# A two-layer decoder trunk: every fifth block of stick-breaking logits takes its PSUM bank from the pool of the transposes

## The chip, the cores and the metric

The kernel runs on one core of a Trainium2 chip. A core has five engines that work through their own instruction queues in order: TensorE (PE; its weight loads, PEld, overlap its matmuls), VectorE (DVE), ScalarE (ACT), GpSimd (POOL) and SyncE (SP), which here only issues DMAs. Matmuls write to PSUM, which holds eight banks of 128 partitions by 512 float32 values. The metric is the device time of one execution in microseconds (us).

## The reference

Two layers over x of 2048 tokens by 1024. Layer 0 projects to four forgetting-attention heads, four stick-breaking heads (both of width 128) and a gate; layer 1 has dilated window attention. The change touches the stick-breaking heads alone. For a block of 128 queries:

```python
strict = jnp.arange(end)[None, :] < qpos[:, None]
z = jnp.einsum('bhqd,bhkd->bhqk', q[:, :, start:end], k[:, :, :end]).astype(jnp.float32)
log_beta = jax.nn.log_sigmoid(z)
log_one_minus = jnp.where(strict, log_beta - z, 0.0)
...
w = jnp.where(strict, jnp.exp(log_beta + later), 0.0)
outs.append(jnp.einsum('bhqk,bhkd->bhqd', w.astype(v.dtype), v[:, :, :end]))
```

Here `later` is, for each key, the sum of `log_one_minus` over all later keys. So a weight is sigmoid(z) of its key times the product of sigmoid(-z) over the later keys of the row: a running product from the last key to the first.

## The kernel before

Every float32 matmul is made of three passes (lines 91 to 93, `mm3`) over operands split into a rounded high part and a low remainder. `split` makes them: ACT copies the high part (L81), DVE subtracts it for the low part (L86).

The function `even_attention` works through 64 units in order: first the stick-breaking heads ("s"), then the forgetting heads ("f"), four heads of each, eight units per head. Unit u holds 2 rows of 128 queries; row i needs the keys up to its own 128, so a unit u has 2 (u // 2 + 1) blocks of at most 512 keys: 2, 2, 4, 4, 6, 6, 8, 8, or 40 blocks per head. In each row the blocks run from the last keys to the first, because the running product is carried that way; the first block of a row is 128 to 512 keys wide, the others 512.

For one block of a stick-breaking head, `qk` takes a PSUM bank, lets PE write the logits into it (L91 to L93, and L878 adds the mask in a row's first block), and then

- ACT writes sigmoid(z) to `rows` (L889) and sigmoid(-z) back into the bank (L890),
- DVE scans the bank from right to left into `rest`, the running product (L893),
- POOL multiplies `rows` by the shifted `rest` (L896), which gives the weights.

The bank is free again after the scan. The generator `pv` of a unit runs two units later, merged with the `qk` of the unit then due: per pair of key tiles it transposes four 128 x 128 pieces of weights into one bank (L928), splits them (L81, L86) and multiplies them by the values into an output bank that it holds for the whole unit; at the end the gate is applied (L946).

The PSUM pool has two kinds of banks, "s" and "t", four each. Before the change all logits use "s"; the transposes and the stick-breaking units' output sums use "t".

The order of the instructions isn't written out. The kernel records its work in the order of the Python code, and a scheduler then orders it for each engine by priority (earlier code first) and by when it thinks operands and free banks are there. Which of a pool's banks a tile gets is decided there too. So a change of a bank's kind can reorder all engines.

Where numbers stand in names (ps_9517), they tell PSUM tiles apart.

Of the kernel before, what the change touches and what calls it, by code (L numbers as in the profile page):

```python
# [831 lines left out]
def even_attention(k, tail):  # L832
    tc, nc = k.tc, k.nc
    c2 = k.c2
    scale = float(P) ** -0.5
    heads, bias = {}, {}

    def load_head(kind, h):
        T, V = (k.fT, k.v["f"]) if kind == "f" else (k.sT, k.v["s"])
        kt = k.big([P, 4, 2, CH], F32R, name="kt")  # L840
        vt = k.big([P, 4, 2, TPC, P], F32R, name="vt")

        def chunk(c):
            s = slice(c * CH, (c + 1) * CH)
            nc.sync.dma_start(kt[:, c].bitcast(F32), T["k"][:, h, :, s].bitcast(F32))
            for z in range(2):
                nc.sync.dma_start(vt[:, c, z].bitcast(F32),
                                  V[s, z, h * P:(h + 1) * P].rearrange("(j p) d -> p j d", p=P).bitcast(F32))

        heads[kind, h] = kt, vt  # L850
        return chunk
# [11 lines left out]
    def qk(kind, h, u, q, tile, left):  # L863

        kt, vt = heads[kind, h]
        c = u // 2
        for i in range(2):
            rows = tile[:, i]
            a = [q[:, z, i * P:(i + 1) * P] for z in range(2)]
            nk = (u * 2 + i + 1) * P  # L870
            carry = None
            for kc in range(c, -1, -1):
                n = CH if kc < c else nk - c * CH
                b = kc * CH
                ps = k.ps("s")
                k.mm3(ps[:, :n], a, [kt[:, kc, z, :n] for z in range(2)], True, kc < c)
                if kc == c:
                    nc.tensor.matmul(ps[:, n - P:n], k.identb, k.after if kind == "f" else k.notbefore,  # L878
                                     start=False, stop=True)
                dst = rows[:, b:b + n]  # L880
                if kind == "f":
                    m = k.small.tile([P, 1], F32, name="m")
                    nc.vector.tensor_tensor_reduce(
                        out=dst, in0=ps[:, :n], in1=bias[h, kc][:, :n], op0=OP.add, op1=OP.max,
                        scale=1.0, scalar=3.0 * NEG if carry is None else carry, accum_out=m)
                    carry = m
                else:

                    nc.scalar.activation(dst, ps[:, :n], AF.Sigmoid, scale=scale)  # L889
                    nc.scalar.activation(ps[:, :n], ps[:, :n], AF.Sigmoid, scale=-scale)  # L890
                    o = left[:, i]
                    back = ps[:, :n][:, ::-1]
                    nc.vector.tensor_tensor_scan(o[:, b:b + n][:, ::-1], back, k.ident[:, :1].to_broadcast([P, n]),  # L893
                                                 1.0 if carry is None else carry, OP.mult, OP.bypass)
                    w = n - 1 if carry is None else n
                    nc.gpsimd.tensor_tensor(dst[:, :w], dst[:, :w], o[:, b + 1:b + 1 + w], op=OP.mult)  # L896
                    carry = o[:, b:b + 1]
                yield
            if kind == "f":
                nm = k.small.tile([P, 1], F32, name="nm")  # L900
                nc.vector.tensor_scalar(nm, carry, -1.0, None, op0=OP.mult)
                den = k.small.tile([P, 2], F32, name="den")
                cuts = [(b, min(b + 2 * CH, nk)) for b in range(0, nk, 2 * CH)]
                for z, (b, e) in enumerate(cuts):
                    nc.scalar.activation(rows[:, b:e], rows[:, b:e], AF.Exp, bias=nm,
                                         accum_out=den[:, z:z + 1])
                if len(cuts) == 2:
                    nc.vector.tensor_tensor(den[:, :1], den[:, :1], den[:, 1:], op=OP.add)
                rd = k.small.tile([P, 1], F32, name="rd")
                nc.vector.reciprocal(rd, den[:, :1])  # L910
                for b, e in cuts:
                    nc.gpsimd.tensor_scalar(rows[:, b:e], rows[:, b:e], rd, 1.0, op0=OP.mult, op1=OP.mult)
# [55 lines left out]
    for n, (kind, h, u) in enumerate(units):  # L968
        rows = k.big([P, 2, S], name="rows")
        rest = k.big([P, 2, S], name="rest") if kind == "s" else None  # L970
        gens = [(qk(kind, h, u, q, rows, rest), 2 * (u // 2 + 1))]
        if n + 1 < len(units):
            q = load_q(*units[n + 1])
        if (kind, h, u) == ("f", 0, 0):
            k.table()
        nxt = order.index((kind, h)) + 1
        if u == 1 and nxt <= 6:
            slopes((nxt - 1) // 2, (nxt - 1) % 2)
        if nxt < len(order) and u >= 3:
            if u == 3:  # L980
                chunk = load_head(*order[nxt])
            else:
                chunk(u - 4)
        if len(past) == 2:
            v = past.pop(0)
            gens.append((pv(*v[0], v[1]), v[0][2] + 1))
        merged(*gens)
        past.append(((kind, h, u), rows))
        if nxt == len(order) and u in (3, 4, 5, 7):

            tail()
# [403 lines left out]
@with_exitstack  # L1395
def tile_hybrid_trunk(ctx, tc, x, even_norm, even_w_in, even_b_f, even_q_gain, even_k_gain, even_w_out,
                      odd_norm, odd_w_in, odd_q_gain, odd_k_gain, odd_w_out, out):
    k = K(ctx, tc)
    k.table()
    x1 = k.dram.tile([S, D], F32, name="x1d")  # L1400
    A = []
    spare = []
    first = left_direct(k, x[0], even_norm, A, spare)
    next(first)
    identity(k)
    late = lambda: constants(k, k.cs, even_norm, odd_norm, even_b_f, even_q_gain, even_k_gain, odd_q_gain, odd_k_gain)
    even_projection(k, x[0], even_w_in[0], first, A, spare, late)
    odd = odd_layer(k, x[0], x1, even_w_out[0], odd_w_in[0], odd_w_out[0], out[0])
    next(odd)
    even_attention(k, lambda: next(odd))  # L1410
    next(odd, None)
# [28 lines left out]
```

## Time and profile before

| what | us |
|---|---|
| median of 3 runs (2764.96 to 2770.11) | 2767.83 |
| the profiled execution's own time | 2767.75 |
| its span, first to last instruction | 2766.0 |
| first scan of a stick-breaking block starts | 701.9 |
| last scan of a stick-breaking block starts | 995.7 |
| 160 scans, 96 of them carried from the block before in the row (L893) | 1.278 each where 512 wide and carried |

The profile is of one execution. Busy times count the instructions of an engine; a wait is the idle time of an engine ahead of an instruction, put down to the instruction that released it. Matmuls are pipelined, so a busy PE isn't a PE at its peak. The chain of waits, followed back from the last instruction, is 70% PE and 17% DVE over the whole span.

### The profile page before, as it was taken

The page shows a single profiled execution, that of the slowest core. Times are in us where ns is not written, and L with a number is a line of the kernel's source. Part 1 is how long each engine was busy: PE and PEld are TensorE (multiplying, and loading weights), DVE is VectorE, ACT ScalarE, POOL GpSimd, SP SyncE. Part 2 cuts the span into 40 slices and gives each one's busy share as a digit, 9 for nine tenths or more (in the row PEclk, how much of TensorE's full clock was granted, in tenths as well). Part 3 has the DMA queues.
Part 4 walks back from the last instruction along what each step waited for, and adds up shares of the span by engine and source line. Part 5 has one row for each costly group of instructions (what it writes and reads, how often), then busy time and mean ns, then how long its engine had stood idle before and what let it go on. Part 6 is the DMA issues. An engine that isn't in the chain of part 4 may idle for free.

```text
span 2766.0 us, 54039 instructions
## 1 busy us (share of the span) xinstructions
PE 2664.9 (96%) x19615; PEld 2418.7 (87%) x19615; DVE 1923.3 (70%) x4255; ACT 1577.2 (57%) x3843; POOL 1102.5 (40%) x903
## 2 busy tenths in 40 slices
PE   6999999999998899999999899999989999999998
PEld 5899878998787789988889899999889999999876
DVE  7867774684788887787237767475896676663976
ACT  6456654454767665665546345555663678665642
POOL 3545654544544433332004654343254432422322
PEclk9999999999999999999999999999999999999999
DMA  5576864445433334443564333444634444444675
GB/s 184 179 214 186 276 209 146 153 143 190 151 115 117 118 116 145 142 132 111 193 203 149 111 108 116 131 133 128 203 98 143 129 154 146 141 138 141 222 257 184
DMA packets 382154, 432.56 MB, mean 156 GB/s; under 512 B 30976, under 2 KB 315968, under 8 KB 381888
## 3 DMA queue, kind: packets, MB, share of 16 engines
q1 hardware_dynamic: 381888, 429.11, 48.3%
q8 instruction: 155, 2.54, 0.4%
q14 instruction: 111, 0.91, 0.1%
HBM read 271.30 MB, written 157.71 MB: 155 GB/s over the span
## 4 chain that ended last, share of the span: by engine, by line
PE 70%; DVE 17%; ACT 5%; DMA 3%; issue 3%; POOL 1%; SPq 1%; DVEq 0%; ACTq 0%; POOLq 0%
PE ps L91 19%; PE ps L93 19%; PE ps L92 19%; DVE rest L893 4%; PE ps L928 3%; PE ps L1237 2%; PE ps L1227 2%; PE ps L1208 2%; PE ps L1153 1%; DVE pT L86 1%; DVE wop L86 1%; DVE c L300 1%; DVE row L1214 1%; PE ps L1200 1%; DVE lp L345 1%
## 5 line engine op out<-in xcount | busy, mean ns | idle before, releaser
L226 POOL TENSOR_TENSOR wraw<-wraw 128x512 f32<-128x512 f32 (+1 forms) x288 | 396.7, 1388 | 417.2 <-DVE wop L86 158.0
L91 PE MATMUL ps<-wop,A 128*128 128x256 f32 (+1 forms) x1856 | 528.5, 285 | 3.8 <-DVE c L300 3.8
L92 PE MATMUL ps<-wop,A 128*128 128x256 f32 (+1 forms) x1856 | 527.2, 284 | 0.0
L93 PE MATMUL ps<-wop,A 128*128 128x256 f32 (+1 forms) x1856 | 525.5, 283 | 0.0
L81 ACT ACTIVATE wop<-wraw 128x512 fp32r<-128x512 f32 (+1 forms) x504 | 315.4, 628 | 339.6 <-PE ps L93 266.0
L86 POOL TENSOR_TENSOR wop<-wraw,wop 128x512 fp32r<-128x512 f32 (+1 forms) x216 | 291.2, 1351 | 494.4 <-ACT wop L81 479.5
L86 DVE TENSOR_TENSOR wop<-wraw,wop 128x512 fp32r<-128x512 f32 (+1 forms) x288 | 234.1, 814 | 239.8 <-ACT wop L81 237.6
L91 PE MATMUL ps<-wop,S 128*128 128x256 f32 x1280 | 369.8, 289 | 4.5 <-DVE c L300 4.5
L92 PE MATMUL ps<-wop,S 128*128 128x256 f32 x1280 | 364.1, 284 | 2.4 <-DVE wop L86 2.4
L93 PE MATMUL ps<-wop,S 128*128 128x256 f32 x1280 | 365.6, 286 | 0.0
L91 PEld LDWEIGHTS ps<-wop,A 128*128 128x128 f32 x1856 | 351.9, 190 | 8.1 <-DVE c L300 4.6
L93 PEld LDWEIGHTS ps<-wop,A 128*128 128x128 f32 x1856 | 352.3, 190 | 1.2 <-issue 0.7
L92 PEld LDWEIGHTS ps<-wop,A 128*128 128x128 f32 x1856 | 352.0, 190 | 0.7 <-issue 0.5
L91 PEld LDWEIGHTS ps<-wop,S 128*128 128x128 f32 x1280 | 242.6, 190 | 8.8 <-issue 8.0
L92 PEld LDWEIGHTS ps<-wop,S 128*128 128x128 f32 x1280 | 243.1, 190 | 4.2 <-DVE wop L86 2.6
L93 PEld LDWEIGHTS ps<-wop,S 128*128 128x128 f32 x1280 | 242.8, 190 | 3.4 <-issue 2.7
L81 ACT ACTIVATE pT<-ps 128x512 fp32r<-128x512 f32 (+2 forms) x352 | 164.7, 502 | 136.8 <-PE ps L928 93.4
L300 DVE TENSOR_TENSOR c<-u,ps 128x512 f32<-128x512 f32 (+1 forms) x242 | 157.4, 656 | 90.3 <-PE ps L93 84.6
L86 DVE TENSOR_TENSOR pT<-ps,pT 128x512 fp32r<-128x512 f32 (+2 forms) x352 | 187.7, 559 | 43.8 <-ACT pT L81 42.3
L896 POOL TENSOR_TENSOR rows<-rows,rest 128x512 f32<-128x512 f32 (+4 forms) x160 | 152.4, 956 | 160.3 <-DVE rest L893 153.1
L1220 ACT ACTIVATE row<-row,nm 128x256 f32<-128x256 f32 (+1 forms) x384 | 172.4, 451 | 64.2 <-DVE nm L1218 60.6
L93 PE MATMUL ps<-A,wop 128*128 128x512 f32 x448 | 177.2, 397 | 4.4 <-DVE ms L104 4.4
(222 smaller groups left out, 6778.3 us busy)
## 6 DMA issues: line engine op xcount, KB each, us to landing
wraw<-in_odd_w_in_dram SPq DMA_DIRECT2D x88, 512.0 KB, 4.0
wraw<-in_even_w_in_dram SPq DMA_DIRECT2D x70, 512.0 KB, 4.2
ld<-qk SPq DMA_DIRECT2D x106, 256.0 KB, 3.1
qk<-c SPq DMA_DIRECT2D x96, 256.0 KB, 2.5
uu<-ot SPq DMA_DIRECT2D x96, 132.0 KB, 1.9
fin<-uu SPq DMA_DIRECT2D x16, 792.0 KB, 4.7
xt<-in_x_dram SPq DMA_DIRECT2D x24, 512.0 KB, 4.5
vv<-c SPq DMA_DIRECT2D x48, 256.0 KB, 2.5
```

The source lines that it names most:

```text
L81: nc.scalar.activation(hi, src, AF.Copy)
L86: (nc.vector if lo_on == "dve" else nc.gpsimd).tensor_tensor(lo, src, hi.bitcast(F32), op=OP.subtract)
L91: mm(out, a[0], b[0], start=start, stop=False, skip_group_check=more)
L92: mm(out, a[0], b[1], start=False, stop=False, skip_group_check=more)
L93: mm(out, a[1], b[0], start=False, stop=stop, skip_group_check=more)
L226: tt = lambda e, o, x, y, op, s: e.tensor_tensor(o[:, s], x[:, s], y[:, s], op=op)
L300: nc.vector.tensor_tensor(out[g], x[g], y[g], op=OP.add)
L893: nc.vector.tensor_tensor_scan(o[:, b:b + n][:, ::-1], back, k.ident[:, :1].to_broadcast([P, n]), 1.0 if carry is None else carry, OP.mult ...
L896: nc.gpsimd.tensor_tensor(dst[:, :w], dst[:, :w], o[:, b + 1:b + 1 + w], op=OP.mult)
L928: nc.tensor.transpose(pt[:, (jx * 2 + i) * P:(jx * 2 + i + 1) * P], rows[:, i, (jj * 2 + jx) * P:(jj * 2 + jx + 1) * P], k.ident)
L1208: nc.tensor.matmul(scores(hp, e), q[pr, za, hp], ring[pr, zb, hp, blocks], start=i == 0, stop=i == 2)
L1220: nc.scalar.activation(row[:, h // 2, h % 2, :nk], row[:, h // 2, h % 2, :nk], AF.Exp, bias=nm[:, h:h + 1], accum_out=ot[:, HW + HG + h:HW ...
```

## The change

Blocks of both kinds of heads are counted as they are recorded, and every fifth block of a stick-breaking head takes a "t" bank in place of an "s" bank:

```diff
     scale = float(P) ** -0.5
     heads, bias = {}, {}
+    blocks = [0]
...
             for kc in range(c, -1, -1):
                 n = CH if kc < c else nk - c * CH
                 b = kc * CH
-                ps = k.ps("s")
+
+                blocks[0] += 1
+                ps = k.ps("t" if kind == "s" and blocks[0] % 5 == 0 else "s")
                 k.mm3(ps[:, :n], a, [kt[:, kc, z, :n] for z in range(2)], True, kc < c)
```

Since the stick-breaking heads come first and have 40 blocks each, these are the blocks 5, 10, ..., 40 of each head, 32 of 160. Blocks 5 and 25 are the first of units 2 and 6 (128 wide); the others are 512 wide. The lines of the changed kernel are three higher from there on (L893 becomes L896). The instructions on PE, DVE, POOL and SP are the same, in another order, from the start of the stick-breaking heads to the first units of the forgetting heads; ACT has two more table loads.

PE, where the second head gives way to the third, before: ps_9467 is the last block of the new head's unit 1, ps_9517 and ps_9526 the first row of its unit 2, ps_9094 and ps_9245 are output sums of the old head.

```order
L91 MATMUL ps_9094<-pT_9211,vt_7696 128x128
L878 LDWEIGHTS identb_688
L878 MATMUL ps_9467<-notbefore_692,identb_688 128x128
L92 MATMUL ps_9094<-pT_9211,vt_7696 128x128
L93 MATMUL ps_9094<-pT_9211,vt_7696 128x128
L91 MATMUL ps_9517<-kt_8635,qT_9369 128x128
L92 MATMUL ps_9517<-kt_8635,qT_9369 128x128
L93 MATMUL ps_9517<-kt_8635,qT_9369 128x128
```

The same block on PE in the changed kernel: ps_9490 holds transposed weights and ps_9377 the output sum of the old head's last unit.

```order
L931 MATMUL ps_9490<-ident_96,rows_9078 128x128 x3
L91 MATMUL ps_9377<-pT_9454,vt_7696 128x256
L92 MATMUL ps_9377<-pT_9454,vt_7696 128x256
L93 MATMUL ps_9377<-pT_9454,vt_7696 128x256
L91 MATMUL ps_9377<-pT_9454,vt_7696 128x256
L92 MATMUL ps_9377<-pT_9454,vt_7696 128x256
L93 MATMUL ps_9377<-pT_9454,vt_7696 128x256
L91 MATMUL ps_9517<-kt_8635,qT_9369 128x128
L92 MATMUL ps_9517<-kt_8635,qT_9369 128x128
L93 MATMUL ps_9517<-kt_8635,qT_9369 128x128
```

The block moved from ahead of the old head's unit 6 to behind most of its unit 7.

DVE at the same head change, before; the scans (L893, which the order names SCALAR_TENSOR_TENSOR) of 128, 256, 512 and 512 are the four of unit 2, and the L86 are low parts of the old head's transposed weights.

```order
L86 TENSOR_TENSOR pT<-ps,pT 128x512 x3
L893 SCALAR_TENSOR_TENSOR rest<-ps,ident 128x128
L893 SCALAR_TENSOR_TENSOR rest<-ps,ident 128x256
L86 TENSOR_TENSOR pT<-ps,pT 128x512
L893 SCALAR_TENSOR_TENSOR rest<-ps,rest,ident 128x512
L86 TENSOR_TENSOR pT<-ps,pT 128x256
L893 SCALAR_TENSOR_TENSOR rest<-ps,rest,ident 128x512
L86 TENSOR_TENSOR pT<-ps,pT 128x512
L86 TENSOR_TENSOR pT<-ps,pT 128x128
L86 TENSOR_TENSOR pT<-ps,pT 128x512
L946 TENSOR_TENSOR gate<-ps,gate 128x256
L86 TENSOR_TENSOR pT<-ps,pT 128x512 x5
```

And in the changed kernel, from the last scan of unit 1 on:

```order
L896 SCALAR_TENSOR_TENSOR rest<-ps,ident 128x512
L86 TENSOR_TENSOR pT<-ps,pT 128x512 x5
L86 TENSOR_TENSOR pT<-ps,pT 128x256
L86 TENSOR_TENSOR pT<-ps,pT 128x128
L86 TENSOR_TENSOR pT<-ps,pT 128x512
L949 TENSOR_TENSOR gate<-ps,gate 128x256
L86 TENSOR_TENSOR pT<-ps,pT 128x512 x6
L86 TENSOR_TENSOR pT<-ps,pT 128x256
L896 SCALAR_TENSOR_TENSOR rest<-ps,ident 128x256
L86 TENSOR_TENSOR pT<-ps,pT 128x128
L896 SCALAR_TENSOR_TENSOR rest<-ps,rest,ident 128x512
L896 SCALAR_TENSOR_TENSOR rest<-ps,ident 128x128
```

The scans of unit 2 moved from among the low parts to behind 15 of them.

ACT at the end of the stage, before: ps_11107 is the last stick-breaking block, and L905 are the first exponentials of the forgetting heads.

```order
L889 ACTIVATE rows_10958<-ps_11107 128x512
L890 ACTIVATE ps_11107<-ps_11107 128x512
L56 ACT_TABLE_LOAD
L81 ACTIVATE pT_11093<-ps_11092 128x256
L905 ACTIVATE rows_11123,den_11203<-rows_11123,nm_11201 128x128
```

And in the changed kernel:

```order
L908 ACT_TABLE_LOAD
L908 ACTIVATE rows_11123,den_11203<-rows_11123,nm_11201 128x128
L81 ACTIVATE pT_11093<-ps_11092 128x128
L908 ACTIVATE rows_11123,den_11254<-rows_11123,nm_11252 128x256
L892 ACT_TABLE_LOAD
L892 ACTIVATE rows_10958<-ps_11107 128x512
L893 ACTIVATE ps_11107<-ps_11107 128x512
L56 ACT_TABLE_LOAD
L908 ACTIVATE rows_11259,den_11360<-rows_11259,nm_11358 128x384
```

The last block's two sigmoids moved behind two exponentials, and each change between the two functions takes a table load.

## The prediction

> **What bounds the kernel now.** I read the page first, then the busy time of each engine in stretches over the part that the change touches, then the waits in that part, then single rows.
>
> ```profile
> span 2766.0 us, 54039 instructions
> PE 2664.9 (96%) x19615; PEld 2418.7 (87%) x19615; DVE 1923.3 (70%) x4255; ACT 1577.2 (57%) x3843; POOL 1102.5 (40%) x903
> L893 DVE TENSOR_TENSOR_SCAN rest<-ps,rest,ident x96: 1258/1278/1284, 709.2 to 995.7; 128x512 f32<-128x512 f32 x96
> 725.00:775.00 50.00, 46.81 (x318) 40.70 (x317) 45.76 (x60) 39.25 (x88) 29.50 (x32) 1.00 0.25 77
> 775.00:800.00 25.00, 22.03 (x141) 18.73 (x139) 16.81 (x27) 13.55 (x33) 7.90 (x9) 0.93 0.49 158
> 800.00:850.00 50.00, 45.91 (x315) 40.32 (x315) 45.21 (x61) 38.33 (x87) 28.63 (x30) 1.00 0.29 86
> 850.00:875.00 25.00, 22.29 (x166) 19.93 (x165) 17.65 (x30) 13.85 (x33) 7.78 (x9) 1.00 0.40 130
> 875.00:925.00 50.00, 45.45 (x304) 39.04 (x304) 46.74 (x62) 38.44 (x87) 30.34 (x31) 1.00 0.35 101
> 925.00:950.00 25.00, 22.51 (x168) 20.35 (x167) 16.61 (x27) 14.08 (x32) 7.37 (x8) 1.00 0.30 95
> 950.00:1000.00 50.00, 45.22 (x301) 38.39 (x300) 46.86 (x71) 39.75 (x88) 28.68 (x30) 1.00 0.38 114
> 1000.00:1025.00 25.00, 25.00 (x205) 23.91 (x204) 18.61 (x52) 14.42 (x32) 3.98 (x5) 1.00 0.46 137
> ```
>
> Over the whole span PE is busy 96%. The stick-breaking heads are the exception: their scans run from about 702 to 998 us, 296 us or a tenth of the span, and there no engine is full. In the stretch rows the columns after the length are the busy times of PE, PE's weight loads, DVE, ACT and POOL. They show two kinds of stretch, in turn, once per head. In the four of 50 us DVE is busy 45.2 to 46.9 us, idle 15.4 us in all: **DVE bounds**. In the three of 25 us, where one head changes to the next, DVE is busy only 16.6 to 17.7 us, while PE is idle 2.97, 2.71 and 2.49 us: **PE bounds**, since there the products of the old head's two longest units are due and the new head's units are short. From 1000 us on PE is full, so what the stage loses or gains up to there reaches the end of the program. What waits in it:
>
> ```profile
> DVE pT L86 <- ACT pT L81: 20.2, 14, 3.2
> DVE rest L893 <- POOL rows L896: 5.9, 10, 0.9
> DVE gate L946 <- PE ps L93: 5.8, 9, 1.8
> DVE rest L893 <- ACT ps L890: 5.7, 6, 3.5
> PEld ps L91 <- DVE rest L893: 25.1, 46, 2.4
> PEld ps L91 <- ACT pT L81: 6.7, 6, 1.8
> PEld ps L92 <- DVE pT L86: 6.6, 8, 1.3
> ```
>
> Total us, times, longest. The row that the change aims at is the fifth: PE's first weight load of a block of logits waits 25.1 us, 46 times, until an earlier scan gives its "s" bank back. But that is PE waiting for DVE. The opposite row, a scan that waits for its logits (the fourth), holds 5.7 us, of which 3.5 are one wait at the start of the stage: 2.2 us remain. DVE's big wait, 20.2 us for the high parts of transposed weights, has nothing to do with banks of logits.
>
> **The change part by part.** No instruction is added to PE, DVE or POOL: 32 of 160 blocks (8 of 40 in each head) get a bank of the other kind, and the scheduler's order follows. The order is the same as before outside this stage.
>
> *Scans moved out of the head changes.* The fifth block of a head is the first of its unit 2 (128 columns, ps_9517 at the second head change). Its bank must now be one of the four that the old head's transposes and output sums are using, so on PE it stands behind nearly all of them, and on DVE all four scans of unit 2 stand behind a run of 15 low-part subtractions (L86); the longest such run was 8. This is so at all three head changes. Durations:
>
> ```profile
> L893 DVE TENSOR_TENSOR_SCAN rest<-ps,rest,ident 128x512 f32<-128x512 f32 x96 | 122.7, 1278 | 5.0 <-ACT ps L890 1.1
> L893 DVE TENSOR_TENSOR_SCAN rest<-ps,ident 128x256 f32<-128x256 f32 x16 | 10.8, 672 | 3.5 <-ACT ps L890 3.5
> L893 DVE TENSOR_TENSOR_SCAN rest<-ps,ident 128x128 f32<-128x128 f32 x16 | 6.7, 416 | 3.9 <-PE ps L928 2.5 <-ACT ps L890 1.0 <-POOL rows L896 0.3
> 857.52 0.42 DVE L946 TENSOR_TENSOR gate<-ps,gate 128x256 f32<-128x256 f32 x1 [0.73 <-PE ps L93]
> 861.11 1.89 DVE L86 TENSOR_TENSOR pT<-ps,pT 128x512 fp32r<-128x512 f32 x3 [3.16 <-ACT pT L81]
> ```
>
> The four scans are 0.416 + 1.278 + 0.672 + 1.278 = 3.64 us. Until now they lay in a stretch where DVE has time (the last two rows: 3.16 us of idle in one piece), free of charge. Moved into the 50 us stretch, where DVE bounds, they add their own length: 3 x 3.64 = **+10.9 us**. The lower end is 0, if they fit into the 15.4 us that DVE still idles in those stretches. I take the upper end, because that idle time is many pieces of a few tenths (scans wait for POOL 5.9 us in 10 pieces, 0.9 at most), which a scan of 1.28 us doesn't fill.
>
> *PE's waits at the head changes.* With the scans gone from there, a low part no longer queues behind a scan, and PE's waits for high and low parts shrink. All that PE idles in the three stretches is 2.97 + 2.71 + 2.49 = 8.2 us; the ends are 0 and -8.2, and I take half, **-4.1 us**, since high parts still wait for ACT and its sigmoids.
>
> *Scans that get their logits earlier.* At most the 2.2 us above; half, **-1.1 us**. PE's 25.1 us are worth no more than this, because the engine that it waits for is the bound where it waits.
>
> *Transposes that wait for a bank with logits.* A block of logits holds its bank until its scan ends; now 32 of them do so among the banks of the transposes. The nearest price is the fifth wait row: 25.1 us over 160 blocks is 0.157 us each, 5.0 us for 32. It counts only where PE bounds, about a third of the stage: **+1.6 us**, with ends 0 and 5.0. Queued behind a waiting transpose on PE stand the products and the next logits; at the head changes nothing on DVE covers that.
>
> *Two more table loads on ACT.* The last stick-breaking block is the 160th, so it also goes to a bank of the other kind, and ACT's order puts its two sigmoids behind the first exponentials of the forgetting heads. That takes two more table loads (one more each at L905 and L889, by the lines of before).
>
> ```profile
> 991.63 0.59 ACT L890 ACTIVATE ps<-ps 128x512 f32<-128x512 f32 x1
> 992.24 1.28 ACT L56 ACT_TABLE_LOAD   x1
> 993.53 0.38 ACT L81 ACTIVATE pT<-ps 128x256 fp32r<-128x256 f32 x1
> 997.06 0.40 ACT L905 ACTIVATE rows<-rows,nm 128x128 f32<-128x128 f32 x1 [3.14 <-DVE nm L901]
> ```
>
> A load occupies ACT for 1.30 us, from the end of the sigmoid at 992.22 to the next copy at 993.53; two are 2.6. ACT idles 3.14 us right behind, waiting for the first row maximum, which can hide them, but the low and high parts of the last units queue behind the loads too: between 0 and +2.6, I take **+1.3 us**. The Trainium skill (ScalarE: Activation LUTs, section "What ACT_TABLE_LOAD costs") gives about 1283 ns for the load and a further 1380 ns for a drain, 2.66 us per switch. Here the load's length agrees and the drain doesn't show: the load starts 0.02 us after the sigmoid's end and the copy 0.01 us after the load's. By the page two switches would be 5.3 us, and half of that would make the sum 1.4 us longer; the row decides.
>
> Sum: 10.9 - 4.1 - 1.1 + 1.6 + 1.3 = **+8.6 us**. The profiled execution took 2767.75 us (span 2766.0 and 1.75 around it), the median of the runs is 2767.83; so 2767.75 + 8.6 = 2776.4 us, +0.31%.
>
> **The rivals.**
>
> *Faster: the moved scans find room.* Decisive is whether DVE's 15.4 us of idle time in the 50 us stretches can take 10.9 us of scans. With logits waiting in five banks rather than four, a scan is always ready when DVE comes free, and the pieces could close up. Then the first term is 0, PE's waits at the head changes go (-8.2), the scans' waits too (-2.2), and the loads hide: -10.4, 2757.4 us. For it: PE really waits 25.1 us for "s" banks. Against it: scans hardly wait for logits (2.2 us), so more logits ahead give DVE little. Chance 0.21.
>
> *No change that can be measured.* Half of the moved scans fit (+5.5), and the two gains (-5.2) cancel them: 2768. For it: both engines are near their limits in this stage (both 90 to 94% busy in the long stretches), so an order can shift waits without shifting the sum. Chance 0.25.
>
> *Worse than forecast: DVE's runs starve PE.* The order on DVE now has four runs of five scans, about 6.4 us each by 5 x 1.278, where inside the heads no run was longer than three full-width scans (3.8 us). During a run no low part is made, and PE can only go on while it has products left. If PE stops for the difference, 2.56 us, at each of the four, and the last two terms take their upper ends (5.0 for 1.6, 2.6 for 1.3), the sum is 8.6 + 10.2 + 3.4 + 1.3 = +23.5, 2791 us. Against it: these runs lie in the stretches where DVE bounds and PE has slack of 3 to 5 us per 50. Chance 0.12.
>
> That the change doesn't do what it says is excluded by the order: 32 blocks stand in banks of the transposes' kind.
>
> **How the numbers follow.** The forecast of 2776.4 has 0.42. The ends of the five terms give -8.2 - 2.2 = -10.4 and 10.9 + 5.0 + 2.6 = +18.5, or 2757 and 2786; I reach to 2789 for part of the worst rival. A run can tell about 0.2% (5.5 us) from no change: faster than 2762 0.21, within 0.25, slower than 2773 0.54 (the forecast and the worst rival).
>
> **What would show it.** In the changed profile, DVE's busy time in the head-change stretches should fall from 17 to about 13.5 us of 25, and the 50 us stretches should become longer by 3 to 4 us each, at the same DVE share. PE's wait for "s" banks (L91 for an L893 scan) should fall well below 25 us, and a wait of PE for low parts (L92 for L86) or of transposes for scans should rise. ACT should show ten table loads for eight, two of them near the end of the stage. I'd be wrong if DVE's share in the long stretches rises above 95% with the scans moved there, or if the head changes become shorter by more than 3 us each; and if time changes outside 700 to 1010 us, the order wasn't the cause.

## The result and the profile after

The changed kernel took 2784.28 us, median of 4 runs (2778.04 to 2784.78), against 2766.81 (4 runs) for the kernel before on the same chip: ratio 1.0053, 95% interval 1.0041 to 1.0065. So it is **slower**, by half a per cent; a ratio of 1 lies outside the interval. One run of a later kernel, 3216.92 us at a granted clock of 0.75 where the others had 0.985 to 0.994, is left out of its median. The profiled execution has a span of 2782.5 us, 16.5 more than before. 14.2 of that lie between the first scan of a stick-breaking head and the last gate of `even_attention`, 603 us before and 617 after; the first scan starts 1.9 us later, though the order of all that runs ahead of it is the same (in the profiles of this study it starts anywhere from 699.8 to 704.4); the rest of the program differs by 0.4.

The page of the changed kernel, its span and first section:

```profile
span 2782.5 us, 53993 instructions
PE 2677.4 (96%) x19615; PEld 2428.1 (87%) x19615; DVE 1925.6 (69%) x4255; ACT 1581.7 (57%) x3845; POOL 1100.6 (40%) x903
```

The work of these engines is the same but for two more instructions on ACT. PE's busy time is 12.5 us longer with as many matmuls, so something made matmuls slower. The next rows, by 310 us of the stage in one stretch, show what. Columns: length, then busy time (and instructions) of PE, PE's weight loads, DVE, ACT and POOL, then the granted clock, the DMA share and GB/s. Before:

```profile
705.00:1015.00 310.00, 283.54 (x1936) 247.99 (x1937) 265.64 (x391) 224.16 (x504) 155.82 (x165) 0.99 0.37 113
```

After:

```profile
705.00:1015.00 310.00, 279.27 (x1822) 240.76 (x1822) 253.47 (x360) 219.64 (x486) 151.71 (x160) 0.96 0.37 112
```

In the same 310 us PE is idle 4.3 us more and also has a lower clock. Busy time times clock, summed over stretches of 5 us so that the rounding matters less, is 281.0 us of full-speed work before and 268.2 after: 12.8 us of work less, 4.3 by idling and the rest by the clock. I call this sum **full-speed PE time** below.

Stretches of the changed kernel, to be held against those of before in the prediction (each head is now about 4 us longer, so they don't line up exactly):

```profile
750.00:775.00 25.00, 21.30 (x130) 18.10 (x129) 18.86 (x26) 14.06 (x33) 12.35 (x13) 0.86 0.17 53
775.00:800.00 25.00, 24.23 (x184) 22.12 (x182) 18.01 (x30) 17.88 (x43) 7.28 (x8) 1.00 0.35 111
...
825.00:850.00 25.00, 21.14 (x126) 18.01 (x126) 19.04 (x25) 13.66 (x32) 12.52 (x12) 0.86 0.16 48
850.00:875.00 25.00, 24.38 (x195) 22.75 (x193) 18.50 (x29) 16.97 (x37) 6.83 (x9) 1.00 0.16 45
...
925.00:950.00 25.00, 24.36 (x169) 22.11 (x169) 13.88 (x23) 14.17 (x32) 4.10 (x5) 0.89 0.13 43
```

PE at the head changes (rows two, four and five) is busy 24.2 to 24.4 us of 25, where it was 22.0 to 22.5. That part got better. The loss stands in the rows just ahead of it, at the end of each head: DVE only 19 us busy, PE 21, and a clock of 0.86. The waits of that part of the changed kernel (total us, times, longest):

```profile
PEld ps L91 <- DVE rest L896: 30.0, 50, 1.8
DVE pT L86 <- ACT pT L81: 24.2, 28, 2.6
PE ps L92 <- DVE pT L86: 10.2, 7, 2.3
DVE rest L896 <- ACT ps L893: 7.9, 7, 3.5
PEld ps L931 <- DVE rest L896: 2.8, 5, 0.6
```

PE's wait for "s" banks, which the change aims at, rose from 25.1 to 30.0 us. Its wait for low parts (the third row) is now 10.2 us, and 9.2 of them are four stops of 2.30 us, one at the end of each head. Before, the same wait held half of that, and its longest pieces stood at the same places: 0.76 us at the end of the first head and 1.1 at the ends of the other three. The wait row and one of these stops, before:

```profile
PE ps L92 <- DVE pT L86: 5.1, 7, 1.1
839.16 0.38 PE L92 MATMUL ps<-pT,vt 128*128 128x256 f32 x1 [1.11 <-DVE pT L86]
```

One of the four in the timeline of the changed kernel (start, length, engine, operation, what it waited for):

```profile
836.16 1.22 DVE L896 TENSOR_TENSOR_SCAN rest<-ps,ident 128x512 f32<-128x512 f32 x1
837.48 4.95 DVE L896 TENSOR_TENSOR_SCAN rest<-ps,rest,ident 128x512 f32<-128x512 f32 x4
842.35 1.86 DVE L86 TENSOR_TENSOR pT<-ps,pT 128x512 fp32r<-128x512 f32 x3
843.07 0.58 PE L92 MATMUL ps<-pT,vt 128*128 128x256 f32 x1 [2.30 <-DVE pT L86]
845.39 0.38 ACT L81 ACTIVATE pT<-ps 128x256 fp32r<-128x256 f32 x1 [4.05 <-PE ps L931]
849.82 1.01 DVE L896 TENSOR_TENSOR_SCAN rest<-ps,ident 128x128 f32<-128x128 f32 x2 [2.62 <-PE ps L93]
```

The first two rows are five scans in a row: from 836.16 to 842.35 DVE makes no low part, PE runs out of products and stops. Then PE is late, ACT waits 4.05 us for it and DVE 2.62 us. The clock in the same place:

```profile
838.40:841.81 3.41, 1.70 (x12) 1.19 (x11) 3.38 (x4) 1.32 (x3) 2.80 (x4) 1.00 0.38 115
841.81:848.64 6.83, 5.57 (x21) 4.65 (x22) 3.12 (x6) 1.49 (x6) 1.71 (x2) 0.50 0.00 0
848.64:852.00 3.36, 3.36 (x28) 3.18 (x27) 2.06 (x3) 1.82 (x4) 1.04 (x2) 1.00 0.55 156
```

The granted clock falls to 0.50 at 841.81, about 1 us after PE has stopped, and stays there for 6.83 us, in which PE is busy for 5.57 us: 2.8 us of full-speed work lost beside the stop. At the ends of the first and third head it is the same length, at the end of the fourth half of it.

What puts five scans in a row? I read the order so: block 35 now needs a bank of the transposes and comes late; the scans of its row, carried from block to block, can't go on, so the scheduler takes the next row's blocks ahead, and when block 35 has its logits the rest of its row is due at once. On DVE's order runs of five scans end at the 39th scan of each head; before, inside a head no run held more than three scans of full width.

### The profile page after: what moved, and what is told of

Its sections match the earlier page's. It is cut to its first block, busy times and chain, and to the rows that moved or that the text cites. A ratio compares the mean times of both kernels' runs of the same rounds, so it can differ in the third digit from the quotient of the medians.

```text
span 2782.5 us, 53993 instructions
## 1 busy us (share of the span) xinstructions
PE 2677.4 (96%) x19615; PEld 2428.1 (87%) x19615; DVE 1925.6 (69%) x4255; ACT 1581.7 (57%) x3845; POOL 1100.6 (40%) x903
## 4 chain that ended last, share of the span: by engine, by line
PE 73%; DVE 15%; ACT 4%; DMA 4%; issue 3%; POOL 1%; SPq 0%; DVEq 0%; ACTq 0%; POOLq 0%
PE ps L91 20%; PE ps L92 20%; PE ps L93 20%; DVE rest L896 3%; PE ps L931 3%; PE ps L1240 2%; PE ps L1230 2%; PE ps L1211 2%; PE ps L1156 1%; DVE wop L86 1%; DVE pT L86 1%; DMA qT<-sqT 1%; DVE row L1217 1%; DVE c L300 1%; PE ps L142 1%
## 5 line engine op out<-in xcount | busy, mean ns | idle before, releaser
L92 PE MATMUL ps<-wop,A 128*128 128x256 f32 (+1 forms) x1856 | 528.4, 285 | 0.0
L86 POOL TENSOR_TENSOR wop<-wraw,wop 128x512 fp32r<-128x512 f32 (+1 forms) x216 | 289.9, 1344 | 493.9 <-ACT wop L81 491.8
L86 DVE TENSOR_TENSOR wop<-wraw,wop 128x512 fp32r<-128x512 f32 (+1 forms) x288 | 232.7, 809 | 240.6 <-ACT wop L81 235.8
L92 PE MATMUL ps<-wop,S 128*128 128x256 f32 x1280 | 365.9, 286 | 2.4 <-DVE wop L86 2.4
L92 PEld LDWEIGHTS ps<-wop,A 128*128 128x128 f32 x1856 | 352.4, 190 | 0.7 <-issue 0.5
L92 PEld LDWEIGHTS ps<-wop,S 128*128 128x128 f32 x1280 | 244.4, 191 | 4.2 <-DVE wop L86 2.7
L86 DVE TENSOR_TENSOR pT<-ps,pT 128x512 fp32r<-128x512 f32 (+2 forms) x352 | 189.1, 560 | 48.2 <-ACT pT L81 46.6
L92 PE MATMUL ps<-pT,vt 128*128 128x256 f32 x576 | 175.6, 306 | 13.1 <-DVE pT L86 11.3
```

Source lines behind the costliest of these rows:

```text
L86: (nc.vector if lo_on == "dve" else nc.gpsimd).tensor_tensor(lo, src, hi.bitcast(F32), op=OP.subtract)
L92: mm(out, a[0], b[1], start=False, stop=False, skip_group_check=more)
```

## The experiments

Every experiment changes only which blocks of logits go to a "t" bank, by this one line. Blocks are counted as in the change: modulo 40 within a head, 160 is the last of all.

```diff
-                ps = k.ps("t" if kind == "s" and blocks[0] % 5 == 0 else "s")
+                ps = k.ps("t" if kind == "s" and COND else "s")
```

Ratios are against the kernel before on the same chip, with 95% intervals; its median there was 2766.81 (with the changed kernel), 2768.81 (the next four), 2769.45 (four more) and 2769.65 us (the last four). "Stage" is the profiled time from the first scan to the last gate, against before. It comes from one profile each: of the two kernels that were profiled twice, one gave +14.2 and +14.7 us, the other +23.8 and +18.7, so differences of less than some 5 us in this column, and in the last one, say little.

| blocks in "t" banks | median us | ratio | stage | full-speed PE time, 705 to 1015 us |
|---|---|---|---|---|
| none (before) | | 1 | | 281.0 |
| every fifth (the change) | 2784.28 | 1.0053 [1.0041, 1.0065] | +14.2 | 268.2 |
| 35 alone | 2776.64 | 1.0028 [1.0017, 1.0040] | +8.0 | 276.2 |
| 5 alone | 2753.77 | 0.9948 [0.9934, 0.9961] | -12.5 | 294.5 |
| 160 alone | 2776.09 | 1.0025 [1.0014, 1.0037] | +5.0 | 272.2 |
| 10, 15, 20, 25, 30 | 2771.22 | 1.0009 [1.0000, 1.0017] | +2.7 | 284.1 |
| fifths but 5 | 2785.93 | 1.0058 [1.0045, 1.0070] | +23.8 | 266.2 |
| fifths but 35 | 2763.83 | 0.9979 [0.9970, 0.9987] | -6.2 | 287.6 |
| fifths but 160 | 2791.31 | 1.0077 [1.0065, 1.0089] | +11.6 | 271.6 |
| fifths but 35 and 40 | 2765.02 | 0.9982 [0.9972, 0.9992] | -5.8 | 290.4 |
| 28 alone | 2768.96 | 1.0003 [0.9994, 1.0012] | +2.5 | 278.7 |
| 9 alone | 2765.36 | 0.9982 [0.9972, 0.9993] | -2.0 | 286.3 |
| the change, again | 2783.36 | 1.0053 [1.0041, 1.0066] | +14.7 | 266.7 |
| fifths but 5, again | 2787.59 | 1.0065 [1.0053, 1.0078] | +18.7 | 268.5 |

**35 alone** (`blocks[0] % 40 == 35`).

> Only block 35 of each head (the second block of unit 7's first row, 4 of 160) takes a "t" bank; the order on DVE then has runs of five scans at blocks 79, 119 and 159, and its longest runs of low parts stay at 8 and 9, as before. Theory A (a run of five scans leaves PE without low parts, and the granted clock falls behind the stall: in the changed kernel PE waits 2.30 us once per head at this place and the clock is 0.66 in the 10 us from 840 on, so 2.30 + 3.4 us per place): 3 or 4 places, +9 to +17 us over before, with the clock low behind each. Theory B (the prediction's: the scans of unit 2 moved out of the head changes): no cost here, within 3 us of before.

(Block 35 is the third block of unit 7's first row, whose blocks are 33 to 36.) Slower by 7.8 us: theory A's direction, a little under its range, and theory B falls. The timeline of this kernel at the end of the second head (the first of the five scans stands just ahead of these four), and the stretches there:

```profile
830.84 5.14 DVE L896 TENSOR_TENSOR_SCAN rest<-ps,rest,ident 128x512 f32<-128x512 f32 x4
836.62 0.58 PE L92 MATMUL ps<-pT,vt 128*128 128x256 f32 x1 [1.11 <-DVE pT L86]
```

```profile
835.00:840.00 5.00, 3.89 (x19) 3.35 (x18) 4.92 (x8) 1.04 (x3) 3.36 (x4) 0.58 0.16 52
840.00:845.00 5.00, 5.00 (x32) 4.63 (x32) 2.52 (x6) 2.94 (x7) 0.80 (x2) 0.74 0.13 36
```

Again a run of five and the fall of the clock. But the stop of PE behind the run, 1.11 us, is as long as the one that the kernel before has at this place. Over 705 to 1015 us PE is busy no less than before (284.98 us against 283.54), and its full-speed time is 4.8 us lower: in this profile the loss is the clock's. It falls at the ends of three heads, before at none of them.

**5 alone** (`blocks[0] % 40 == 5`).

> Only block 5 of each head (the first of unit 2) takes a "t" bank; DVE then has runs of 13 to 14 low parts at the head changes as in the changed kernel (15), and no run of five scans. Theory B: +8 to +11 us over before (3 x 3.64 us of scans moved, less PE's waits). Theory A: within 3 us of before, and the granted clock no lower than before's.

Faster by 15 us. Both theories' forecasts miss, and B's has the wrong sign. This is also the fastest kernel of the study, faster than the kernel before and the changed one. It moves the same four scans per head that the first term of the prediction is about, behind 13 or 14 low parts. The head changes of this kernel:

```profile
775.00:800.00 25.00, 24.09 (x174) 21.54 (x172) 22.59 (x35) 19.34 (x45) 12.23 (x14) 1.00 0.71 210
850.00:875.00 25.00, 24.08 (x173) 21.36 (x171) 22.45 (x35) 19.68 (x46) 12.68 (x14) 1.00 0.72 215
925.00:950.00 25.00, 24.10 (x172) 21.40 (x171) 23.17 (x36) 19.97 (x47) 12.69 (x15) 1.00 0.77 225
```

PE idles 0.9 us in each where it idled 2.5 to 3.0, and the clock is 1.00. A head takes 73.8 us, from the gate at 849.00 to the one at 922.84, against 77.9 before. Before, ACT made eight sigmoids of the next head's unit 3 in one piece ahead of the old head's high parts:

```profile
856.68 0.49 ACT L889 ACTIVATE rows<-ps 128x384 f32<-128x384 f32 x1 [1.26 <-POOL rows L896]
...
859.95 0.61 ACT L890 ACTIVATE ps<-ps 128x512 f32<-128x512 f32 x1
860.46 1.58 ACT L81 ACTIVATE pT<-ps 128x512 fp32r<-128x512 f32 x3
861.11 1.89 DVE L86 TENSOR_TENSOR pT<-ps,pT 128x512 fp32r<-128x512 f32 x3 [3.16 <-ACT pT L81]
861.13 0.39 PE L91 MATMUL ps<-pT,vt 128*128 128x256 f32 x1 [1.59 <-ACT pT L81]
```

DVE's 3.16 us, which the prediction read as room for scans, was a wait in the chain that feeds PE. With block 5 held back the sigmoids stand behind the old head's high parts, and the stretches at the same place are full:

```profile
848.00:853.00 5.00, 5.00 (x45) 5.00 (x44) 3.58 (x6) 2.38 (x5) 0.00 (x0) 1.00 0.17 52
853.00:858.00 5.00, 5.00 (x44) 4.96 (x43) 3.90 (x8) 3.40 (x9) 0.64 (x1) 1.00 0.13 39
```

**160 alone** (`blocks[0] == 160`).

> Only the last block of the last stick-breaking head takes a "t" bank; the order of the scans stays that of before, and ACT has the two more table loads. Theory C (the loads and the late last block cost time of their own, since the last head in the changed kernel lost about 6 us where the others lost 3.5): +2.6 to +5 us. Theories A and B: 0 to +1.3 us, since the forgetting heads give PE other work there.

Slower by 7.3 us, above every range. The order of every engine equals that of before up to this last block, so what the edit does must show at the end of the stage. ACT and DVE there, and the last 30 us in one stretch, of this kernel:

```profile
1001.14 1.28 ACT L908 ACT_TABLE_LOAD   x1 [0.17 <-DVE nm L904]
1002.95 1.28 ACT L892 ACT_TABLE_LOAD   x1
1005.35 1.28 ACT L56 ACT_TABLE_LOAD   x1
```

```profile
996.27 2.67 DVE L896 TENSOR_TENSOR_SCAN rest<-ps,rest,ident 128x512 f32<-128x512 f32 x2
1005.36 1.28 DVE L896 TENSOR_TENSOR_SCAN rest<-ps,rest,ident 128x512 f32<-128x512 f32 x1 [2.23 <-ACT ps L893]
```

```profile
985.00:1015.00 30.00, 25.05 (x165) 21.93 (x165) 24.09 (x55) 21.93 (x44) 13.71 (x16) 0.94 0.18 54
```

The last scan starts 6.4 us behind the end of the scan ahead of it, and PE and its clock lose with it: before, PE was busy 27.54 us in these 30 at a clock of 1.00, 4.0 us more of full-speed work (2.5 by idling, 1.5 by the clock). That is most of the 5.0 us of the stage. What the median has beyond it isn't explained by the edit's order. ("The seam" below is this place, where ACT goes over from the stick-breaking to the forgetting heads.)

**10 to 30** (`blocks[0] % 40 in (10, 15, 20, 25, 30)`).

> Blocks 10, 15, 20, 25 and 30 of each head take a "t" bank, and 5, 35 and 40 stay in "s"; DVE's runs of low parts are then the 8 of before, table loads 8, and the only runs of five scans stand at the start of the stage. If the loss comes from blocks 5, 35 and 40 alone (A, B and C): within 4 us of before, and faster by 1 to 5 us if earlier logits are worth anything. If "t" banks with logits cost the transposes time anywhere (a rival, D): slower by 3 to 8 us.

Slower by 2.4 us, at the limit of what can be told: within the first expectation, just below the rival's. These five blocks per head do little without the others.

**Fifths but 5** (`blocks[0] % 40 in (10, 15, 20, 25, 30, 35, 0)`) and, below, the same again with the changed kernel beside it.

> All fifth blocks but block 5 of each head take a "t" bank. DVE's runs of low parts at the head changes are 8, 11 and 11; runs of five scans, the seam and the ten table loads stay as in the changed kernel (2784 us). Theory B (the prediction's) said that block 5 costs: 8 us faster than the changed kernel. Theory E (after block 5 alone gained 15 us: its gain is also in the changed kernel, and the other seven blocks cost some 30): 8 to 15 us slower than the changed kernel, 2792 to 2799. If the runs of five scans take the gain away (theory F): within 4 us of it.

> The changed kernel itself, once more on the same chip as the run without block 5 that stands beside it, to compare them like with like: every theory expects 12 to 18 us slower than before.

> The changed kernel without block 5 (all other fifth blocks stay), once more beside the changed kernel on the same chip. If block 5's gain acts inside the changed kernel too: 5 to 15 us slower than the changed kernel beside it. If the gain of block 5 is taken away there by the other blocks: within 3 us of it.

The first time it stood 1.7 us above the changed kernel's median, taken on another occasion, as theory F expected; theories B and E miss. Beside the changed kernel it is 4.2 us slower. That is between the two expectations, and the intervals overlap. So inside the change block 5 gains a few us at most, where alone it gains 15: most of its gain is lost in the company of the others.

**Fifths but 35** (`blocks[0] % 40 in (5, 10, 15, 20, 25, 30, 0)`).

> All fifth blocks but block 35 of each head take a "t" bank: runs of 15 low parts stay, one run of five scans is left, table loads 8 (the order of the last block changes with it). Theory A (the runs of five scans and the clock behind them are the loss): 12 to 25 us faster than the changed kernel, 2759 to 2772, with the granted clock back at 0.99. Theory D (many blocks in "t" banks cost the transposes time): no better than 2778.

Theory A's forecast holds: 20 us faster than the change and 5.6 faster than before. The five-scan runs at the heads' ends are gone, PE's wait for low parts (L92) falls from 10.2 to 1.9 us, and the loss of clock is gone too. The stretch of this kernel, and of the changed one, over the same 265 us:

```profile
750.00:1015.00 265.00, 247.21 (x1733) 217.96 (x1732) 226.40 (x347) 190.66 (x420) 126.43 (x134) 1.00 0.36 107
```

```profile
750.00:1015.00 265.00, 237.97 (x1571) 206.58 (x1569) 212.40 (x306) 180.42 (x399) 123.40 (x130) 0.95 0.33 100
```

9.2 us of idling, as much as the four stops of 2.30, and 5% of the clock, 12 us of 238: together about the 20 us. Not all of it need be block 35's own: though block 160 still has its "t" bank here, the order at the seam is that of before again, with eight table loads, and alone that seam cost 7.3 us.

**Fifths but 160** (`blocks[0] % 5 == 0 and blocks[0] < 160`).

> All fifth blocks but the very last take a "t" bank: table loads 8, everything else in the scans' order as in the changed kernel. Theory C (the seam costs its own time, 7 us when alone): 2775 to 2780. If the loads hide behind what the runs of five scans lose there anyway: within 3 us of the changed kernel, 2781 to 2787.

Neither: 2791.31 us, slower than the change. The stage is 2.6 us shorter than in the change, which one profile each can't tell from nothing. But the end of the program, some 1250 us after the stage, takes 10.7 us longer than before (from ACT's last instruction of line 305 on). In the trace ACT and DVE have another order there, from about 2640 us on, which none of the other kernels has. So this edit reordered a second place as well, and it doesn't tell what the seam costs inside the change.

**Fifths but 35 and 40** (`blocks[0] % 40 in (5, 10, 15, 20, 25, 30)`).

> Blocks 5, 10, 15, 20, 25 and 30 of each head take a "t" bank, 35 and 40 stay in "s": runs of 14 low parts, table loads 8. If only 35 and 40 cost and block 5 gains: 2752 to 2762, as with block 5 alone. If the four middle blocks cost what the kernel with blocks 10 to 30 showed (2.4 us) or more together with block 5: 2756 to 2768.

2765.02 us, the second expectation. Against 5 alone it adds 10 to 30 and is 11 us slower, though these cost only 2.4 by themselves. The parts of this change don't add up.

**28 alone** (`blocks[0] % 40 == 28`).

> Only block 28 of each head takes a bank with the transposes (condition: block number modulo 40 equal to 28; the change's own blocks are left out). VectorE's order then has three runs of five scans in a row, as with block 35 alone, and its runs of low-part subtractions at the head changes stay at 8, as before. Theory A (a block taken late from the other pool lets the next row's blocks pass, the run of five scans stops TensorE for over 2 us and the granted clock falls behind the stop, wherever in the head it stands): 4 to 12 us slower than before, and a 5-us window with a granted clock below 0.8 behind each run. Rival (block 35 costs because it stands at the head's end, beside the head change): within 3 us of before, clock above 0.9 behind the runs.

The rival's time holds: no change. The timeline has the run of five (here split by a gate, with one scan ahead of it), and right behind it PE is fed:

```profile
817.48 5.22 DVE L896 TENSOR_TENSOR_SCAN rest<-ps,rest,ident 128x512 f32<-128x512 f32 x4
```

```profile
815.00:820.00 5.00, 5.00 (x34) 4.25 (x32) 4.93 (x6) 4.40 (x9) 3.87 (x4) 1.00 0.22 70
820.00:825.00 5.00, 4.27 (x25) 3.25 (x24) 4.87 (x6) 4.49 (x12) 3.28 (x3) 1.00 0.14 39
825.00:830.00 5.00, 5.00 (x36) 4.41 (x36) 4.90 (x7) 4.55 (x10) 3.29 (x4) 1.00 0.00 0
```

This run stands before unit 7's eight blocks, and in these 15 us PE stops for no longer than 0.42 us at a time. Why is argued, not tested: PE has the logits of unit 7 and the products of an earlier unit to go on with, while at the end of a head the blocks to come are short and the products wait for DVE. The clock does fall in this kernel too (0.50 for 3.41 us from 835.85), but at the head's end, 13 us behind the run and next to the stop of 1.11 us that the kernel before has as well. Its full-speed PE time in the window is 2.3 us below that of before, and the ratio shows no loss of time.

**9 alone** (`blocks[0] % 40 == 9`).

> Only block 9 of each head (the first block of the head's unit 3) takes a bank with the transposes. VectorE's runs of low-part subtractions at the head changes become 12 long (8 before, 13 and 14 with block 5 alone), and there is no run of five scans. Theory G (what gains is that scans and sigmoids of the next head's early units no longer stand inside the old head's chain from state to state at the head change, whichever block brings it about): 5 to 15 us faster than before, with TensorE busier in the 10 us behind the old head's last gates. Rival (block 5 gains for another reason of its own): within 3 us of before.

Faster by 4.3 us, just below theory G's range and above the rival's; behind the old head's last gate PE is busy for all of 10 us (871.70 to 881.70), before for 9.43 (872.80 to 882.80). This kernel holds back unit 3 in place of unit 2. In its timeline sigmoids still stand ahead of the old head's high parts (857.43 to 860.43), and PE still stops there:

```profile
861.08 0.38 PE L91 MATMUL ps<-pT,vt 128*128 128x256 f32 x1 [1.05 <-ACT pT L81]
```

That agrees with theory G, in which the sigmoids in the old head's chain are what costs, but a kernel that moves the sigmoids alone was not made.

## Why the prediction came out right, and where its steps were wrong

The direction was right and the time lies inside the range, but the change costs twice the forecast (+8.6 us forecast, +16.5 by span and +17.5 by medians), and not for the reasons given. That was luck: the largest term of the sum has the wrong sign in the runs, and the largest loss was in no term.

- **Scans moved out of the head changes, +10.9 us: wrong sign.** Block 5 alone moves them and gains 15 us; inside the change it still doesn't cost. The step took DVE as the bound of the long stretches and charged the scans there at full length. They found room: a head shrank from 77.9 to 73.8 us with 3.64 us more of scans behind the head change. That was the first rival, priced at -10.4 and given 0.21 because DVE's idle pieces are short. The longest of these pieces, 3.16 us at the head change, was a wait for ACT, and PE waited with it.
- **PE's waits at the head changes, -4.1: right sign, too small.** In the changed kernel they fell from 8.2 to 2.0 us (0.77, 0.62 and 0.64 in the three rows), in that with block 5 alone to 2.7. The reason for taking half (high parts wait for ACT's sigmoids) fell away with block 5 alone, since the sigmoids moved as well.
- **Scans that get their logits earlier, -1.1: wrong, small.** Their wait for logits rose from 5.7 to 7.9 us.
- **Transposes that wait for a bank with logits, +1.6: about right.** They wait 2.8 us in 5 waits, between the ends of 0 and 5.0.
- **Two more table loads, +1.3: too small.** They are there, 1.28 us each as priced. Alone the block costs 4.0 us of PE work at the end of the stage and 7.3 by medians. What goes beyond the upper end of 2.6 is the delay of the last scan, which the term left out, and a part that stays open.
- **What was left out of the sum was the largest piece.** Of the 12.8 us of full-speed PE time lost from 705 to 1015 us, 4.3 are idling and 8.5 the clock, which was in no term and no rival. The rival "DVE's runs starve PE" had 0.12, with four runs of 5 x 1.278 us and four added stops of 2.56 us, 10.2 in all. The trace shows the four runs and four stops of 2.30, but before there were already shorter ones at these places: PE's wait for low parts rose by 5.1 us, from 5.1 to 10.2. I gave the rival little because PE has 3 to 5 us of slack per 50. Slack averaged over a stretch is no cover for a stop at one place in it: with block 28 the runs are as long and cost nothing, with block 35 they stand at the heads' ends and the kernel is 7.8 us slower, and leaving 35 out of the change saves 20.
- **Signs.** The head's period grew by 3.7 us (77.9 to 81.6), inside the 3 to 4 us that the prediction named as its proof, through another cause. Two signs spoke against its steps: PE's wait for "s" banks is 30.0 us and not well below 25, and DVE's busy time in the head-change stretches is 18.0, 18.5 and 13.9 us, where about 13.5 was forecast for all three. Ten table loads and more waiting for low parts came as forecast.

So without the others block 5 gains 15 us, and 35, 160 and the five middle blocks lose. These four add up to +2.5 us (7.8 - 15.0 + 7.3 + 2.4), while the change costs 13.7 by medians in the repeat: 11 us come from the parts together. Why the gain at the head change is lost in the company of the others was not found.

## What to carry to other kernels

Before counting an engine's idle time as room for other work, ask which instruction it waits for, and whether the bound engine waits for the same one: then moving that instruction can gain more than filling the room. Price a run of one kind of work on a feeding engine at the place where it falls, by what the fed engine still has queued there, not by slack averaged over a stretch. Where blocks are assigned to pools by a count, try the blocks one by one: one of eight gained 15 us alone, and with the others that gain was lost.

## What the hardware showed unexpectedly

The length of a stop of PE doesn't price it. In all fourteen profiles the granted clock is 1.00 or 0.50, and between 690 and 1020 us it stays at 0.50 for 3.41 us or for 6.83, whatever the stop. The falls stand on a grid of 3.41 us in each trace, and they follow what PE did in the 3.41 us ahead of them. In the changed kernel PE was busy for 1.70 of them (quoted above). At the same head's end with block 35 alone it was busy for 1.92, with a stop of only 1.11 us, and the clock fell for as long; before, with the same stop, it was busy for 2.18, and the clock stayed. Block 35 alone, then before:

```profile
832.38:835.79 3.41, 1.92 (x13) 1.30 (x11) 3.31 (x3) 2.61 (x8) 3.08 (x3) 1.00 0.39 115
835.79:842.62 6.83, 6.00 (x25) 5.60 (x26) 4.75 (x9) 1.19 (x4) 3.23 (x4) 0.50 0.11 38
```

```profile
837.07:840.48 3.41, 2.18 (x16) 1.94 (x17) 3.31 (x5) 0.66 (x2) 2.18 (x2) 1.00 0.32 99
840.48:843.89 3.41, 3.41 (x28) 3.07 (x27) 3.41 (x8) 2.47 (x6) 2.06 (x3) 1.00 0.02 5
```

From 700 to 1015 us in these traces the clock always fell where PE was busy for less than 1.77 of the 3.41 us, never where it was busy for more than 2.3, and between them both happened. So how a thin stretch of PE work lies on the grid counts too, and I take a part of these times to be chance: "fifths but 5", profiled twice, has its falls at other places in each, and stages 5.1 us apart. The Trainium skill (TensorE: Matmul & The Clock Gate, Part 1) says that the clock has two states, half and full, and drops after at least one idle window of about 3.4 us. The rows agree with the two states and with the length of the window. They don't agree that it has to be idle: PE was busy for half of it, and its longest stop was 2.30 us.
